# Turning attention queries by 32x32 blocks and on-chip transfers instead of on TensorE (fp32 decoder trunk, one core)

## The chip, the core and the metric

One core of one Trainium2 chip. The metric is the device time of one execution in microseconds; the time before is the median of three runs. Engines are named as the profile names them: PE (TensorE), DVE (VectorE), ACT (ScalarE), POOL (GpSimd) and SP (SyncE, which here only issues transfers).

## The reference, cut to what matters

A decoder trunk on 512 tokens of width 1024 in fp32: one Griffin layer (gated linear recurrence and a SwiGLU), then one layer of dilated attention, and a second SwiGLU. The change lies in the attention layer:

```python
k, v = shared_kv(h, kv_norm, w_kv, k_norm, cos, sin)      # 3 groups x 2 key/value heads x 128

q = (rms_norm(h, b_norm) @ w_q).reshape(B, S, N_GROUPS, Q_HEADS, HEAD_DIM)   # 3 groups x 8 heads x 128
q = rms_norm(q, q_norm[:, None, :])         # over each head's 128
q = apply_partial_rope(q, cos, sin)         # the first 32 of the 128
for g, (window, dilation) in enumerate(((128, 1), (512, 4), (2048, 16))):
    o, l = dilated_window_attention(q[:, :, g], k[:, :, g], v[:, :, g], window, dilation)
wts = softmax(stack(lses)); o = sum(wts * outs)
h = h + o.reshape(B, S, 1024) @ w_o
```

A query meets some 128 keys of each of the three groups, and the groups share one softmax.

## The kernel before

Weights are fp32 and are used as two parts, a high one (rounded to the format fp32r) and a low one (the rest), and so are activations: every product is three matmuls, hi x hi, lo x hi and hi x lo (`mm3`, lines 163 to 165). `Stream` brings the weights in pieces of 128x1024. `_load` issues the load on SP's queue into one of two raw buffers `wr` (line 100). `_split` makes the high part `wh` on ACT (line 117). The low part `wl` comes in one of two ways: for plain pieces DVE subtracts (line 124); for pieces of the kind "dma" ACT writes the weights negated and rounded (line 120) and POOL issues a transfer that adds the weights from memory to them (line 121), which leaves the rest. All 28 pieces of the query weights `w_q` are of the kind "dma" (4 of the 24 are loaded a second time). A load waits until the piece two before it has been split.

`project` goes through four pieces per pass and, with each, over four tiles of 128 tokens: 24 matmuls a piece, 96 a pass (lines 1048 to 1050), and each tile ends in one PSUM bank of 128 tokens x 512 (four heads). Twelve pieces give keys and values. Then `project_q(0)` makes the queries of the first key/value head in three passes (g = 0, 1, 2), pieces 136 to 147 of the stream, and `project_q(1)` those of the second in four (its third pass goes over half the tiles at a time).

For a finished tile `collect` multiplies by the norm's gain (DVE, line 982, into a buffer `kn`), squares (ACT, line 984), sums over each head (DVE, line 985) and queues the rotary step. `normed` computes the norm's factors for the pass and scales each tile (DVE, line 1014). `turn` transposes the four 128x128 heads of a tile on PE (line 1127) into one PSUM bank, and ACT copies the bank into `qt` (line 1129) with the tokens regrouped in four phases. `query_part` splits `qt` into `qh` and `ql` (`halve`: ACT line 279, DVE line 280). These steps are not done at once: `at(n, fn)` sets one n steps later, and `tick()` after each tile of a projection (or each second step of attention) carries out what is due. The order of instructions on each engine is that of the program, with `tc.high_priority()` around the splits and the softmax.

`attend` runs 32 units (2 key/value heads x 4 blocks of 128 tokens x 4 phases). A unit is `scores` (9 matmuls into a bank called S or X), `softmax` (DVE 1192 and 1195, ACT 1200, DVE 1201, POOL 1202), then three units later `turned` (PE transposes, line 1214) and `values`. `plan` says how much of the remaining projection and of the output projection stands between the units; `START_Q` steps of `project_q(1)` come before the first. While `filling[0]` is true all scores use the bank S.

The second SwiGLU and the first already turn their rows without PE, in `land`: DVE transposes 32x32 blocks (line 720), and transfers on SP (12) and POOL (4) put the blocks where they belong (line 730).

Of the kernel before, what the change touches and what calls it, by code (L numbers as in the profile page):

```python
# [15 lines left out]
F32 = mybir.dt.float32  # L16
# [4 lines left out]
ALU = mybir.AluOpType  # L21
# [135 lines left out]
def trunk(tc, A, out):  # L157
# [695 lines left out]


N_TMP = 6
N_KN = 4
STATS = 5
N_PR = 4
LAG = 3
START_Q = 10  # L860


def rotary(nc, A, rp, tp):
# [79 lines left out]
def attention(tc, A, ap, ws, env):  # L943
# [12 lines left out]
    def phases(t):  # L956
        return t.rearrange("q (p n i) -> q p n i", n=4, p=4)

    sph = ap.tile([128, T], F32, name="sph", tag="kn", bufs=N_KN)
# [14 lines left out]
    def collect(raw, nh, j, n, st, tab, g_row):  # L974

        if j == 0:
            st["sq"] = ap.tile([128, n * nh], F32, name="sqc", tag=f"sqc{nh}").rearrange("q (t i) -> q t i", i=nh)
            st["kn"] = []
        dst = ap.tile([128, 512], F32, name="kn", tag="kn", bufs=N_KN)
        rows = raw[:, :128 * nh]  # L980
        x = dst.rearrange("q (h d) -> q h d", d=128)[:, :nh]
        V.tensor_tensor(x, rows.rearrange("q (h d) -> q h d", d=128),
                        grow[:, g_row].unsqueeze(1).to_broadcast([128, nh, 128]), ALU.mult)
# [15 lines left out]
    def normed(st, nh, tab, turn, lag, tiles=range(4)):  # L999

        kn = dict(zip(tiles, st["kn"]))
        first, n = tiles[0], len(tiles)

        def factors():
            sq = st["sq"]
            V.scalar_tensor_tensor(sq, sq, 1.0 / 128.0,
                                   epsv[:, tab + first:tab + first + n].unsqueeze(2).to_broadcast([128, n, nh]),
                                   ALU.mult, ALU.add)
            st["r"] = rsqrt(sq.rearrange("q t i -> q (t i)"), ap, f"qr{nh}")

        def scale(t):
            j = nh * (t - first)
            x = kn[t].rearrange("q (h d) -> q h d", d=128)[:, :nh]
            V.tensor_tensor(x, x, st["r"][:, j:j + nh].unsqueeze(2).to_broadcast([128, nh, 128]), ALU.mult)
# [46 lines left out]
    v2h, v2l = (ap.tile([128, 2, 512], F32R, name=n, tag=n, bufs=1) for n in ("ph", "pl"))  # L1061
    xph, xpl = [], []
    for k in range(KB):
        tags = (("qt", 12), ("qt", 12)) if k < 6 else (("qh", 3), ("ql", 3))
        for lst, src, (tag, bufs), eng in ((xph, xh, tags[0], S.copy), (xpl, xl, tags[1], G.tensor_copy)):
            lst.append(ap.tile([128, T], F32R, name="xp", tag=tag, bufs=bufs))
            eng(phases(lst[k]), by_phase(src[k].bitcast(F32)))
    at(STATS, stats)
    ws.asp = 2
    for g in range(3):  # L1070
# [45 lines left out]
    def project_q(kv):  # L1116

        early, late, every = range(2), range(2, 4), range(4)
        passes = [(0, every), (1, every), (2, early), (2, late)] if kv else [(g, every) for g in range(3)]
        for j, (g, tiles) in enumerate(passes):  # L1120
            def done_q(t, ps, g=g, st={}, tiles=tiles, j=j):
                collect(ps, 4, t - tiles[0], len(tiles), st, t, 3 + g)
                if t == tiles[-1]:
                    def turn(j, rows):
                        pt = bank("X" if kv and g else "PT")
                        for i in range(4):
                            PE.transpose(pt[:, 128 * i:128 * i + 128], rows[:, 128 * i:128 * i + 128], ident)  # L1127
                        q = ap.tile([128, 4, 4, 32], F32, name="qt", bufs=12)
                        S.copy(q, pt.rearrange("q (h p i) -> q p h i", h=4, p=4))
# [19 lines left out]
    def query_part(kv, n, g):  # L1149
# [5 lines left out]
        halve(qt.pop((n, kv, g)).rearrange("q p h i -> q (p h i)"), qh, ql)  # L1155
        qs_[kv, n, g] = qh, ql

    def query_parts(kv, n):
# [134 lines left out]
    for k, u in enumerate(attend()):  # L1293
        for i, (fill, steps, u0, u1) in enumerate(plan):
# [90 lines left out]
```

## Time and profile before

| | |
|---|---|
| Runs | 1169.56, 1167.65, 1168.88 us; median 1168.88 |
| Profiled execution | 1166.22 us, span 1164.4 us, mean granted clock of PE 0.999 |
| PE, PE weight load | 1151.9 us (99%), 952.2 us (82%) |
| DVE, ACT, POOL | 851.5 us (73%), 623.8 us (54%), 186.3 us (16%) |
| First load of query weights, first scaling of queries | 538.4 us, 587.5 us |
| Query transposes on PE, line 1127 | 96, 14.4 us busy |

Times in the profile run from the start of the span. In a group's row, "x96 | 14.4, 274 | 1.4 <-ACT" reads: 96 instructions, busy 14.4 us in all, 274 ns each, and the engine sat idle 1.4 us ahead of them, mostly until that ACT instruction. A row of waits reads: who waited, for whom, us in all, times, longest. A row of a queue gives min/median/max of an issue in ns and the first and last start in us.

### The profile page before, as it was taken

The numbers are of one execution on the slowest core, as the hardware profiler recorded it, in microseconds if no ns is written. First come the engines' busy times: TensorE is split into PE (matmuls) and PEld (weight loads), VectorE is DVE, ScalarE is ACT, GpSimd is POOL, SyncE is SP. The second block draws the span as 40 slices with busy tenths as digits, with TensorE's granted clock in tenths as the row PEclk, the third lists the DMA queues.
The fourth block names the chain that finished last, engine by engine and source line by source line (L and its number), as shares of the span: only waits on it lengthen the run. The fifth ranks groups of instructions, "written<-read, shape, count | busy, mean of one in ns | idle before, by whom it ended". The sixth has DMA issues, their size and how long they took to land.

```text
span 1164.4 us, 15128 instructions
## 1 busy us (share of the span) xinstructions
PE 1151.9 (99%) x5403; PEld 952.2 (82%) x5403; DVE 851.5 (73%) x1525; ACT 623.8 (54%) x901; POOL 186.3 (16%) x221
## 2 busy tenths in 40 slices
PE   9999999999999999999999999999999999999998
PEld 6788888888888888888888888798888888888887
DVE  7988688968777676887565667765988777676864
ACT  6797455543435353565555667665555435353532
POOL 4210010201011000020411334341002011011000
PEclk9999999999999999999999999999999999999999
DMA  7643366966665723433978657534668665757323
GB/s 244 149 114 110 105 225 159 242 193 160 183 164 174 188 73 82 129 107 89 222 182 178 142 113 179 127 73 108 219 160 233 186 165 177 182 162 191 81 71 128
DMA packets 92234, 179.61 MB, mean 154 GB/s; under 512 B 8704, under 2 KB 27008, under 8 KB 92160
## 3 DMA queue, kind: packets, MB, share of 16 engines
q1 hardware_dynamic: 72720, 130.80, 34.6%
q0 software_dynamic: 18864, 47.19, 22.9%
q8 instruction: 43, 0.70, 0.2%
q10 hardware_dynamic: 576, 0.66, 0.2%
q14 instruction: 31, 0.25, 0.1%
HBM read 164.99 MB, written 2.10 MB: 143 GB/s over the span
## 4 chain that ended last, share of the span: by engine, by line
PE 92%; DVE 3%; ACT 2%; issue 1%; DMA 1%; POOL 0%; ACTq 0%; DVEq 0%; SPq 0%
PE ps L165 25%; PE ps L164 25%; PE ps L163 25%; PE ps L1048 5%; PE ps L1049 5%; PE ps L1050 5%; PE ps L1127 1%; PE ps L1214 1%; DVE xc L451 1%; DMA h<-in_x 0%; ACT pr L1200 0%; PE ps L296 0%; DVE ql L280 0%; ACT wh L117 0%; DMA wr<-in_w_in 0%
## 5 line engine op out<-in xcount | busy, mean ns | idle before, releaser
L117 ACT CAST wh<-wr 128x1024 fp32r<-128x1024 f32 (+2 forms) x136 | 131.2, 969 | 136.3 <-PE ps L164 83.1
L164 PE MATMUL ps<-wl,xh 128*128 128x512 f32 x320 | 124.7, 390 | 0.0
L165 PE MATMUL ps<-wh,xl 128*128 128x512 f32 x320 | 124.7, 390 | 0.0
L163 PE MATMUL ps<-wh,xh 128*128 128x512 f32 x320 | 124.7, 390 | 0.0
L165 PE MATMUL ps<-gh,wl 128*128 128x512 f32 x288 | 114.6, 398 | 0.3
L163 PE MATMUL ps<-gh,wh 128*128 128x512 f32 x288 | 113.8, 395 | 0.0
L164 PE MATMUL ps<-gl,wh 128*128 128x512 f32 x288 | 113.7, 395 | 0.0
L124 DVE TENSOR_TENSOR wl<-wr,wh 128x1024 fp32r<-128x1024 f32 (+2 forms) x93 | 100.0, 1083 | 17.4 <-ACT wh L117 17.0
L649 POOL DMA_DIRECT2D S<-in_f_in x40 | 48.2, 1237 | 370.8 <-DMA S<-in_f_in 187.2
L163 PE MATMUL ps<-xh,wh 128*128 128x512 f32 x256 | 101.1, 396 | 0.7 <-ACT xh L274 0.7
L663 ACT CAST wh<-S 128x1024 fp32r<-128x1024 f32 x60 | 63.0, 1050 | 70.4 <-PE ps L165 28.0
L164 PE MATMUL ps<-xl,wh 128*128 128x512 f32 x256 | 100.2, 391 | 0.1
L165 PE MATMUL ps<-xh,wl 128*128 128x512 f32 x256 | 100.0, 391 | 0.0
L664 DVE TENSOR_TENSOR wl<-S,wh 128x1024 fp32r<-128x1024 f32 x60 | 73.2, 1222 | 31.5 <-ACT wh L663 31.5
L163 PE MATMUL ps<-wh,T 128*128 128x512 f32 x240 | 93.6, 390 | 0.0
L165 PE MATMUL ps<-wh,T 128*128 128x512 f32 x240 | 93.6, 390 | 0.0
L164 PE MATMUL ps<-wl,T 128*128 128x512 f32 x240 | 93.5, 390 | 0.0
L1048 PE MATMUL ps<-wh,xh 128*128 128x512 f32 x224 | 91.6, 409 | 0.0
L1050 PE MATMUL ps<-wh,xl 128*128 128x512 f32 x224 | 87.8, 392 | 0.0
L1049 PE MATMUL ps<-wl,xh 128*128 128x512 f32 x224 | 87.4, 390 | 0.0
L781 DVE TENSOR_TENSOR h<-h,ps 128x512 f32<-128x512 f32 x64 | 43.3, 685 | 54.9 <-PE ps L165 54.9
L163 PEld LDWEIGHTS ps<-wh,xh 128*128 128x128 f32 x320 | 60.1, 188 | 12.6
(284 smaller groups left out, 2669.7 us busy)
## 6 DMA issues: line engine op xcount, KB each, us to landing
S<-in_f_in SPq DMA_DIRECT2D x40, 512.0 KB, 6.4
S<-in_f_in POOLq DMA_DIRECT2D x40, 512.0 KB, 8.9
wr<-in_f_out SPq DMA_DIRECT2D x36, 512.0 KB, 5.2
wr<-in_w_q SPq DMA_DIRECT2D x28, 512.0 KB, 6.9
wl<-in_w_q POOLq DMA_DIRECT2D x28, 512.0 KB, 7.6
GA<-in_f_in SPq DMA_DIRECT2D x20, 512.0 KB, 4.9
GB<-in_f_in SPq DMA_DIRECT2D x20, 512.0 KB, 6.9
UB<-in_f_in SPq DMA_DIRECT2D x20, 512.0 KB, 4.9
```

What stands on the lines that cost most here:

```text
L117: nc.scalar.copy(hi[:, c], r[:, c])
L124: a = eng.tensor_tensor(lo[:, c], r[:, c], hi[:, c].bitcast(F32), ALU.subtract)
L163: PE.matmul(ps, wh, xh, start=first, stop=False, skip_group_check=on)
L164: PE.matmul(ps, wh, xl, start=False, stop=False, skip_group_check=on)
L165: PE.matmul(ps, wl, xh, start=False, stop=last, skip_group_check=on)
L649: nc.gpsimd.dma_start(c, p.part(1, q, n == "S1", i), accum_op=ALU.add)
L663: S.copy(hi, r)
L664: V.tensor_tensor(lo, r, hi.bitcast(F32), ALU.subtract)
L781: V.tensor_tensor(by_time(x), by_time(x), in_turn(ps), ALU.subtract)
L1048: PE.matmul(ps[t], xh[k][:, r], wh[:, c], start=k == 0, stop=False)
L1049: PE.matmul(ps[t], xh[k][:, r], wl[:, c], start=False, stop=False)
L1050: PE.matmul(ps[t], xl[k][:, r], wh[:, c], start=False, stop=k == 7)
```

## The change

Four things change together.

1. *Turning.* For queries, `collect` writes its tile with the four heads' 32-wide blocks side by side (block b, head h, 32). `scale_heads` scales on ACT, one instruction for each head (4 per tile, 96 in all). `turn_blocks` transposes the 32x32 blocks of a tile on DVE in place (24). When the second tile of a pair is done, `turn` issues 16 transfers from SBUF to SBUF for the pair: each takes 32 partitions x 2 tiles x 128 values (32 KB), 12 on SP's queue and 4 on POOL's. Twelve pairs make 144 and 48. The 96 PE transposes, the 24 ACT copies out of PSUM and the 24 DVE scalings are gone. `query_part(0, 0, g)` is set eight steps behind the transfers.
2. *Buffers.* `kn` and `qt` hold pairs: `kn` has two buffers of two tiles (before, four of one), `qt` six of two (before, twelve of one).
3. *Low parts.* Of the first twelve pieces of `w_q` every second one gets its low part by DVE's subtraction: six ACT passes and six accumulating POOL transfers go, six DVE subtractions come.
4. *Order.* `START_Q` is 13, not 10; the third pass of `project_q(0)` is normalised in halves; `filling[0]` ends with the first entry of `plan`, so that scores alternate between S and X from there on.

```diff
-    p_q = add_pieces([A["w_q"][i] for i in (*range(24), *range(20, 24))], "dma")
+    p_q = add_pieces([A["w_q"][i] for i in range(12)], "dma", 2)
+    add_pieces([A["w_q"][i] for i in (*range(12, 24), *range(20, 24))], "dma")
...
-N_KN = 4
+N_KN = 2
...
-START_Q = 10
+START_Q = 13
...
-        dst = ap.tile([128, 512], F32, name="kn", tag="kn", bufs=N_KN)
+        if j % 2 == 0:
+            st["pairs"].append(ap.tile([128, 2, 512], F32, name="kn", tag="kn", bufs=N_KN))
+        dst = st["pairs"][-1][:, j % 2]
...
+            x = dst.rearrange("q (b h d) -> q b h d", b=4, h=nh)
+            V.tensor_tensor(x, rows.rearrange("q (h b d) -> q b h d", b=4, h=nh),
+                            g.rearrange("q (b d) -> q b d", b=4).unsqueeze(2).to_broadcast([128, 4, nh, 32]), ALU.mult)
...
+        def scale_heads(t):
+            x = kn[t].rearrange("q (b h d) -> q h b d", b=4, h=nh)
+            for i in range(nh):
+                j = nh * (t - first) + i
+                S.activation(x[:, i], x[:, i], AF.Copy, scale=st["r"][:, j:j + 1])
+
+        def turn_blocks(t):
+            blocks = kn[t].rearrange("q (k i) -> q k i", i=32)
+            V.transpose(blocks, blocks)
+            if t % 2:
+                turn(t - 1, st["pairs"][(t - first) // 2])
...
-            at(2 + j, lambda t=t: scale(t))
-            at(lag + j, lambda t=t: turn(t, kn[t]))
+            if lag:
+                at(2 + j, lambda t=t: scale(t))
+                at(lag + j, lambda t=t: turn(t, kn[t]))
+            else:
+                at(2 + j, lambda t=t: scale_heads(t))
+                at(3 + j, lambda t=t: turn_blocks(t))
...
+                if not kv and g == 2:
+                    tiles = (early, late)[t // 2]
...
-                    def turn(j, rows):
-                        pt = bank("X" if kv and g else "PT")
-                        for i in range(4):
-                            PE.transpose(pt[:, 128 * i:128 * i + 128], rows[:, 128 * i:128 * i + 128], ident)
-                        q = ap.tile([128, 4, 4, 32], F32, name="qt", bufs=12)
-                        S.copy(q, pt.rearrange("q (h p i) -> q p h i", h=4, p=4))
-                        qt[j, kv, g] = q
-                        if not kv and not j:
-                            query_part(0, 0, g)
-
-                    normed(st, 4, 0, turn, {3: 7}.get(j, 8), tiles)
+                    def turn(n, rows):
+                        q = ap.tile([128, 2, 4, 128], F32, name="qt", tag="qt", bufs=6)
+                        src = rows.rearrange("q n (b x) -> q n b x", b=4)
+                        for p in range(4):
+                            for b in range(4):
+                                (G if p == 3 else nc.sync).dma_start(q[32 * b:32 * b + 32, :, p],
+                                                                     src[32 * p:32 * p + 32, :, b])
+                        for i in range(2):
+                            qt[n + i, kv, g] = q[:, i]
+                        if not kv and not n:
+                            at(8, lambda: query_part(0, 0, g))
+
+                    normed(st, 4, 0, turn, None, tiles)
...
+                if i == 0 and given[i] == steps:
+                    filling[0] = False
                 if i == 1 and given[i] == steps:
                     move()
-                if i == 2 and given[i] == steps:
-                    filling[0] = False
```

What stands where on the engines that wait or are waited for: SP's queue where the first two query groups are turned (`wr146` is the load of piece 146), before:

```order
L100 DMA wr144_5063<-in_w_q 128x1024
L100 DMA wr145_5108<-in_w_q 128x1024
L100 DMA wr146_5191<-in_w_q 128x1024
L100 DMA wr147_5230<-in_w_q 128x1024
L100 DMA wr148_5279<-in_w_q 128x1024
L100 DMA wr149_5324<-in_w_q 128x1024
L100 DMA wr150_5407<-in_w_q 128x1024
L100 DMA wr151_5446<-in_w_q 128x1024
```

and in the changed program:

```order
L100 DMA wr145_5111<-in_w_q 128x1024
L1163 DMA qt_4995<-kn_4891 32x2x128 x12
L1163 DMA qt_5042<-kn_4922 32x2x128 x12
L100 DMA wr146_5192<-in_w_q 128x1024
L100 DMA wr147_5262<-in_w_q 128x1024
L100 DMA wr148_5311<-in_w_q 128x1024
L100 DMA wr149_5346<-in_w_q 128x1024
L100 DMA wr150_5448<-in_w_q 128x1024
L1163 DMA qt_5229<-kn_5125 32x2x128 x12
L1163 DMA qt_5276<-kn_5156 32x2x128 x12
L100 DMA wr151_5528<-in_w_q 128x1024
```

Two blocks of 24 transfers now stand in the row of loads, the first ahead of `wr146`, the second ahead of `wr151`.

PE at the beginning of attention, where the names `kh` and `kl` (4011 to 4013 for the three groups) mark the scores of a unit (9 rows each) and lines 1048 to 1050 (1075 to 1077 in the changed program) the projection. Before, projection follows on the first unit's last scores:

```order
L163 MATMUL ps<-kh_4012,qh 128x64
L164 MATMUL ps<-kl_4018,qh 128x64
L165 MATMUL ps<-kh_4012,ql 128x64
L163 MATMUL ps<-kh_4013,qh 128x64
L164 MATMUL ps<-kl_4019,qh 128x64
L165 MATMUL ps<-kh_4013,ql 128x64
L1048 MATMUL ps<-wh_5409,xh 128x512
L1049 MATMUL ps<-wl_5410,xh 128x512
L1050 MATMUL ps<-wh_5409,xl 128x512
```

In the changed program the first unit's last scores are followed by those of the second and the third:

```order
L163 MATMUL ps<-kh_4013,qh 128x64
L164 MATMUL ps<-kl_4019,qh 128x64
L165 MATMUL ps<-kh_4013,ql 128x64
L163 MATMUL ps<-kh_4011,qh 128x128
L164 MATMUL ps<-kl_4017,qh 128x128
L165 MATMUL ps<-kh_4011,ql 128x128
L163 MATMUL ps<-kh_4012,qh 128x64
L164 MATMUL ps<-kl_4018,qh 128x64
L165 MATMUL ps<-kh_4012,ql 128x64
L163 MATMUL ps<-kh_4013,qh 128x64
L164 MATMUL ps<-kl_4019,qh 128x64
L165 MATMUL ps<-kh_4013,ql 128x64
```

The projection between the first units has moved ahead of them, and three units follow on one another in the bank S.

DVE where a group of queries ends: in the changed program the turning of the pairs `kn_4891` and `kn_4922` stands here ahead of the gain multiplication of the next group, into a pair that takes the buffer of `kn_4891` (`wl144` is the low part of piece 144, by subtraction):

```order
L1035 STREAM_TRANSPOSE kn_4891<-kn_4891 128x512 x2
L1035 STREAM_TRANSPOSE kn_4922<-kn_4922 128x512
L124 TENSOR_TENSOR wl144_5080<-wr144_5077,wh144_5079 128x1024
L1035 STREAM_TRANSPOSE kn_4922<-kn_4922 128x512
L992 TENSOR_TENSOR kn_5125<-ps_4964,grow_1855 128x512
L281 TENSOR_TENSOR ql_5102<-qt_4995,qh_5101 128x512
```

The multiplication in the fifth row is new behind the transfers out of `kn_4891`.

More of the change, by code (lines that the diff above doesn't have):

```diff
@@ L957, in phases @@
         return t.rearrange("q (p n i) -> q p n i", n=4, p=4)
-    sph = ap.tile([128, T], F32, name="sph", tag="kn", bufs=N_KN)
+    sph = ap.tile([128, 2 * T], F32, name="sph", tag="kn", bufs=N_KN)[:, :T]
     G.tensor_copy(phases(sph), by_phase(ssum))
@@ L976, in collect @@
         if j == 0:
-            st["sq"] = ap.tile([128, n * nh], F32, name="sqc", tag=f"sqc{nh}").rearrange("q (t i) -> q t i", i=nh)
-            st["kn"] = []
-        dst = ap.tile([128, 512], F32, name="kn", tag="kn", bufs=N_KN)
-        rows = raw[:, :128 * nh]
-        x = dst.rearrange("q (h d) -> q h d", d=128)[:, :nh]
-        V.tensor_tensor(x, rows.rearrange("q (h d) -> q h d", d=128),
-                        grow[:, g_row].unsqueeze(1).to_broadcast([128, nh, 128]), ALU.mult)
+            st["sq"] = ap.tile([128, 16], F32, name="sqc", tag=f"sqc{nh}")[:, :n * nh].rearrange(
+                "q (t i) -> q t i", i=nh)
+            st["kn"], st["pairs"] = [], []
+        if j % 2 == 0:
+            st["pairs"].append(ap.tile([128, 2, 512], F32, name="kn", tag="kn", bufs=N_KN))
+        dst = st["pairs"][-1][:, j % 2]
+        rows = raw[:, :128 * nh]
+        g = grow[:, g_row]
+        if nh == 2:
+            x = dst.rearrange("q (h d) -> q h d", d=128)[:, :nh]
+            V.tensor_tensor(x, rows.rearrange("q (h d) -> q h d", d=128),
+                            g.unsqueeze(1).to_broadcast([128, nh, 128]), ALU.mult)
+        else:
+            x = dst.rearrange("q (b h d) -> q b h d", b=4, h=nh)
+            V.tensor_tensor(x, rows.rearrange("q (h b d) -> q b h d", b=4, h=nh),
+                            g.rearrange("q (b d) -> q b d", b=4).unsqueeze(2).to_broadcast([128, 4, nh, 32]), ALU.mult)
+            x = x[:, 0]
         S.activation(rows, rows, AF.Square)
@@ L1063, in attention @@
     for k in range(KB):
[L1064 to L1067, printed above, removed]
+        if k < 6:
+            pair = ap.tile([128, 2, T], F32R, name="xp", tag="qt", bufs=6)
+            homes = [pair[:, i] for i in range(2)]
+        else:
+            homes = [ap.tile([128, T], F32R, name="xp", tag=tag, bufs=3) for tag in ("qh", "ql")]
+        for lst, src, home, eng in ((xph, xh, homes[0], S.copy), (xpl, xl, homes[1], G.tensor_copy)):
+            lst.append(home)
+            eng(phases(home), by_phase(src[k].bitcast(F32)))
     at(STATS, stats)
@@ L1120, in project_q, with done_q @@
         for j, (g, tiles) in enumerate(passes):
[L1121 removed]
+            def done_q(t, ps, g=g, sts=({}, {}), tiles=tiles):
+                if not kv and g == 2:
+                    tiles = (early, late)[t // 2]
+                st = sts[tiles == late]
                 collect(ps, 4, t - tiles[0], len(tiles), st, t, 3 + g)
                 if t == tiles[-1]:
[L1124 to L1134 removed]
+                    def turn(n, rows):
[10 more added lines that the diff above has]
+                    normed(st, 4, 0, turn, None, tiles)
             yield from project(p_q + 12 * kv + 4 * j, xh, xl, done_q, tiles)
@@ L1154, in query_part @@
         qh, ql = [ap.tile([128, 512], F32R, name=x, tag=x, bufs=tags[2]) for x in tags[:2]]
-        halve(qt.pop((n, kv, g)).rearrange("q p h i -> q (p h i)"), qh, ql)
+        halve(qt.pop((n, kv, g)).rearrange("q p x -> q (p x)"), qh, ql)
         qs_[kv, n, g] = qh, ql
```

1 line of the change is left out of this document (added).

## The prediction

> **What bounds the kernel now.** I read the page's head and its chain first (which engine ends last), then PE's waits, then the windows of the stretch in which the queries are made, then the rows of the queues that the change touches.
>
> ```profile
> span 1164.4 us, 15128 instructions
> PE 1151.9 (99%) x5403; PEld 952.2 (82%) x5403; DVE 851.5 (73%) x1525; ACT 623.8 (54%) x901; POOL 186.3 (16%) x221
> ...
> PE 92%; DVE 3%; ACT 2%; issue 1%; DMA 1%; POOL 0%; ACTq 0%; DVEq 0%; SPq 0%
> ```
>
> PE is busy 99% of the span and carries 92% of the chain: an instruction taken from PE shortens the time by its own length, unless PE then waits. The windows (PE, PEld, DVE, ACT, POOL busy, clock, DMA share, GB/s) show where there is room for new waits:
>
> ```profile
> 580.00:600.00 20.00, 20.00 (x97) 16.59 (x96) 10.20 (x32) 10.77 (x15) 2.58 (x3) 1.00 0.86 198
> 660.00:680.00 20.00, 19.44 (x124) 16.96 (x123) 10.36 (x37) 11.58 (x24) 7.62 (x6) 1.00 0.63 128
> 700.00:720.00 20.00, 18.22 (x120) 15.95 (x119) 12.67 (x37) 14.45 (x25) 8.20 (x6) 1.00 0.74 165
> 720.00:740.00 20.00, 19.04 (x128) 16.82 (x126) 15.08 (x48) 17.25 (x33) 8.27 (x7) 1.00 0.71 159
> ```
>
> At 580 to 600 (projection of the first queries alone) PE never stops and DVE and ACT are half free; from 660 on attention is woven in, POOL works, and PE idles a little. The second row of this fence shows PE's waits on what the change replaces:
>
> ```profile
> PE ps L1127 <- ACT qt L1129: 1.3, 2, 1.0
> ...
> PE ps L163 <- ACT qt L1129: 1.2, 1, 1.2
> ```
>
> **Removed from PE.** 96 transposes and those waits. Their own row gives 14.4 us; what they cost in the pipe I take from the collecting pass, which is periodic, and from the matmuls inside it.
>
> ```profile
> L1127 PE MATMUL ps<-ident,kn 128*128 128x128 f32 x96 | 14.4, 274 | 1.4 <-ACT qt L1129 1.3
> ...
> 601.13 0.69 DVE L982 TENSOR_TENSOR kn<-ps,grow 128x512 f32<-128x512 f32 x1 [7.64 <-PE ps L1050]
> 624.78 0.69 DVE L982 TENSOR_TENSOR kn<-ps,grow 128x512 f32<-128x512 f32 x1 [7.64 <-PE ps L1050]
> ...
> 605.23 0.39 PE L1049 MATMUL ps<-wl,xh 128*128 128x512 f32 x1
> 614.30 0.40 PE L1050 MATMUL ps<-wh,xl 128*128 128x512 f32 x1
> ```
>
> One pass (96 matmuls and 16 transposes) lasts 624.78 - 601.13 = 23.65 us. The last two rows are the first and the last of 41 back-to-back matmuls: 9.07 / 40 = 0.227 us each, so 96 take 21.77 and 16 transposes 1.88. Six passes' worth: **-11.3 us** (14.4 is the other end). The waits: 1.3 + 1.2 = **-2.5**. Together -13.8. A piece of weights (24 matmuls) is then 5.44 us of PE.
>
> **Moved on ACT, DVE, POOL.**
>
> ```profile
> L120 ACT ACTIVATE wl<-wr 128x1024 fp32r<-128x1024 f32 x26 | 27.6, 1060 | 16.7 <-PE ps L1049 16.6
> ...
> L1014 DVE TENSOR_TENSOR kn<-kn,qr4y 128x512 f32<-128x512 f32 x24 | 15.7, 706 | 0.2
> ...
> L1129 ACT COPY qt<-ps 128x512 f32<-128x512 f32 x24 | 13.7, 581 | 15.4 <-PE ps L1127 15.2
> ...
> L279 ACT CAST kh<-ps 128x128 fp32r<-128x128 f32 x24 | 6.3, 265 | 8.5 <-DVE kl L280 4.9 <-PE ps L1102 3.6
> ...
> L720 DVE STREAM_TRANSPOSE wt<-e 128x512 f32<-128x512 f32 x40 | 25.9, 687 | 0.0
> ...
> L124 DVE TENSOR_TENSOR wl<-wr,wh 128x1024 fp32r<-128x1024 f32 x71 | 85.9, 1220 | 13.8 <-ACT wh L117 13.6
> ```
>
> ACT loses 24 copies (13.9) and 6 low-part passes (6.4) and gains 96 scalings of 128x128, at the nearest row's 0.265: +25.4, net +5.1 us over some 190. DVE loses 24 scalings (16.9) and gains 24 transposes (16.5) and 6 subtractions (7.3), net +6.9. POOL loses 6 accumulating transfers and gains 48 small ones. I cost all three at nothing while projection runs alone, since DVE and ACT are half idle there; at 720 to 740 ACT has 2.75 of 20 us left, and if that cover fails the 16 scalings per pass show: that is in the last term below. The two buffers of paired rows mean that DVE's gain multiplication of the next group waits until the last pair has landed; queued behind it are the low parts of piece 146 on, which PE reaches at 581.3 + 6 x 5.44 = 614, and PE has other banks until then.
>
> **Added to SP: the term that decides.** Twelve pairs, each 12 transfers on SP and 4 on POOL, go into the queue that also carries the weight loads, in order.
>
> ```profile
> L730 SPq DMA_DIRECT2D gl<-wt x96: 591/599/927, 227.3 to 1087.7; - x96
> ...
> L730 POOL DMA_DIRECT2D gl<-wt x32: 549/572/608, 227.9 to 1082.7; - x32
> DMA to landing us min/median/max: 2.0/2.2/3.8
> ```
> ```profile
> 227.30 8.11 SPq L730 DMA_DIRECT2D gl<-wt  x12
> 235.45 0.59 SPq L93 DMA_DIRECT2D wr<-in_f_out  x1
> ```
> ```profile
> L647 SPq DMA_DIRECT2D S<-in_f_in x40: 367/462/3014, 157.7 to 1047.6; - x40
> ```
> ```profile
> L93 SPq DMA_DIRECT2D wr<-in_f_out x36: 367/469/2145, 158.8 to 1121.5; - x36
> ```
>
> The nearest transfers in kind (L730, on chip, four 512-byte runs on each of 32 partitions) take 0.60 each, 0.64 with the gap. The new ones have two runs on each of 32. The row nearest in that is L647, two runs per partition, median 0.46. Bounds of c, one issue with its gap: 0.37 (its minimum) to 0.64. I take c = 0.50, L647's median and L730's gap of 0.04, because runs per partition are what the two rows differ in beside the place.
>
> When do they start? ACT's row below marks the start of piece 140 (581.3), which ends the first query group; DVE has the factors at 587.5:
>
> ```profile
> 581.33 1.06 ACT L120 ACTIVATE wl<-wr 128x1024 fp32r<-128x1024 f32 x1 [0.23 <-PE ps L1049]
> ...
> 587.51 2.50 DVE L1014 TENSOR_TENSOR kn<-kn,qr4y 128x512 f32<-128x512 f32 x4
> ```
>
> Two tiles scaled on ACT (8 x 0.265), the second one's DVE transpose (0.69) and 0.8 of gaps put the first transfer at 591.1. A group's 24 transfers take 24c, and the loads of pieces 146 and 147 stand behind them (146 is one of the six whose low part DVE now subtracts, with no transfer; it is there in time). Then each load waits for the split of the load two before it: 146, 148, 150, then the second group's 24 transfers, then 151. With L from issue to landing of a load, A the same for an accumulating low part, and 8.3 for splits and issues between them (two on ACT, 2.1, three times; the POOL issue, 0.9; gaps, 1.1), piece 151 is ready at 591.1 + 48c + 3L + A + 8.3. PE wants it at 581.3 + 11 x 5.44 = 641.2.
>
> ```profile
> wr<-in_w_q SPq DMA_DIRECT2D x28, 512.0 KB, 6.9
> wl<-in_w_q POOLq DMA_DIRECT2D x28, 512.0 KB, 7.6
> ...
> wr<-in_w_kv SPq DMA_DIRECT2D x12, 512.0 KB, 3.5
> ```
> ```profile
> L121 POOL DMA_DIRECT2D wl<-in_w_q x28: 860/874/1382, 548.7 to 722.5; - x28
> ...
> DMA to landing us min/median/max: 5.8/7.4/9.8
> ```
>
> L lies between 3.5 (loads alone) and 6.9 (with accumulates beside them); behind a pause of the loads it is between, 5.2. A: between its minimum 5.8 and its median 7.4, 6.6. So 591.1 + 24 + 15.6 + 6.6 + 8.3 = 645.6 less 641.2: near **+4.4** of stalls up to there (none at c = 0.37 with L = 4, 17.0 at c = 0.64 with the medians).
>
> **Scores in one bank.** Attention begins three steps later, with the turned queries eight steps behind their transfers. By the order, the first three units' scores come late and back to back in one PSUM bank (before, projection lay between). PE waits twice until DVE has read the bank:
>
> ```profile
> 707.50 0.42 DVE pr L1192
> 707.97 0.48 DVE pr L1195
> ```
>
> 0.9 each, **+1.8** (0 if the rest hides it). **Later blocks** stand between loads whose pieces last longer, since attention lies between them; with ACT's lost cover I take **+1.5**, half of 0 to 3.
>
> **Sum.** -13.8 + 4.4 + 1.8 + 1.5 = -6.1. The profiled execution is 1166.2 (span 1164.4), so 1160.1; it lies 2.7 below the median 1168.9, to which I compare: **about 1163**. 0.2% (2.3 us) is what a measurement of this kernel can tell.
>
> The Trainium skill, "VectorE: DVE Perf Modes", section "Rules for kernel authors", speaks against the change: a 128x128 transpose belongs on TensorE if PSUM may take the result, since VectorE turns only 32x32 blocks. The price of the detour is here the transfers; the rival of a full SP queue below is that rule's outcome.
>
> **Rivals.**
> 1. *All hidden.* c near 0.37 and L near 4: piece 151 is ready at 591.1 + 17.8 + 12 + 6.6 + 8.3 = 635.8, before PE wants it. -13.8 with 0 to 1.8 for the scores: some 1156. For it: L647's minimum, and loads that land in 3.5 when alone. Against: that row's median, 0.46.
> 2. *Cancelled.* c = 0.55 with L = 6.2: 651.0, a stall of 9.8; with 1.8 and 1.5 the sum is -0.7: 1168.
> 3. *The SP queue becomes the bound (slower).* The transfers cost what L730 costs (0.64), since both are on chip, and loads land in 6.2: 591.1 + 30.7 + 18.6 + 7.0 + 8.3 = 655.7, a stall of 14.5; later blocks 3, scores 1.8: +5.5, 1174. It decides from a stall of about 10.5 at piece 151 on. For it: L730's minimum and median are alike, so its price does not look like a queue's. Against: the load right behind L730's twelve took as long, 0.59, where its like (L93) takes 0.47 in the median, so part of the price is the queue's.
>
> A stall in one piece of over 3.4 us would by the Trainium skill ("TensorE: Matmul & The Clock Gate", Part 1) halve PE's clock for about as long. No window above has such a gap (clock 1.00 with 1.78 us idle in 20). In rival 3 two such stalls would, as an estimate from that page, add some 3 us.
>
> That the change does not do what it says is not open: the 96 transposes are gone from PE's order.
>
> **Chances.** Likeliest (1159 to 1166.5): 0.35. All hidden (below 1159): 0.24. Cancelled (within 0.2%): 0.18. SP's queue (above 1171.2): 0.23. Faster 0.35 + 0.24 = 0.59. The range leaves out a tenth at each end: 1154.5 (everything hidden and the transposes nearer 14.4) to 1174. The likeliest one's own range is 1159 to 1166.5.
>
> **What would show it.** PE's row of transposes on the identity for queries gone, and a pass of 21.8 us where projection runs alone; SP's row of the new transfers at 0.46 (0.33 for rival 1, 0.60 for rival 3); PE waiting on the low parts of pieces 147 to 151 for 3 to 6 us in all; waits of scores on DVE of about 1.8; PE's clock still 1.00. The prediction is wrong if the new transfers cost 0.6 and PE does not wait (the loads have more slack than I give them), or if PE waits for the turned queries or for ACT at 700 to 760.

## The result: 3.1% slower

The changed kernel takes 1204.2 us in the median (1202.4 to 1205.5) beside 1168.3 for the kernel before: ratio 1.0307, 95% interval 1.0288 to 1.0327. Forecast was 1163, with 1174 as the upper end. In the experiments below, one execution each of e5 and e8 took 4070 and 3468 us, and their medians leave it out. The page of the profiled execution (span, busy times, PE's granted clock in 40 slices, the chain):

```profile
span 1200.5 us, 15374 instructions
...
PE 1161.7 (97%) x5307; PEld 955.9 (80%) x5307; DVE 859.5 (72%) x1540; ACT 631.6 (53%) x967; POOL 208.3 (17%) x263
...
PEclk9999999999999999999998799799999999999999
...
PE 79%; issue 5%; DVE 4%; SPq 4%; DMA 4%; ACT 2%; POOL 1%; ACTq 0%; DVEq 0%; POOLq 0%
```

The span grew by 36.1 us, and two rows split it. PE's idle time (span less busy) went from 12.5 to 38.8: +26.3. PE's busy time went up by 9.8 although 96 transposes, 11.3 us by the prediction's price, are gone: the remaining matmuls took 21.1 us longer. 26.3 + 21.1 - 11.3 = 36.1. The clock row shows why matmuls took longer. Before, it was 9 in every slice:

```profile
PEclk9999999999999999999999999999999999999999
```

The mean granted clock agrees: 0.982 beside 0.999, and 0.017 of 1200.5 us is 20 us. The same in windows (PE, PEld, DVE, ACT, POOL busy, clock, DMA share, GB/s), first two of before, then the changed kernel's:

```profile
620.00:640.00 20.00, 20.00 (x93) 16.56 (x92) 11.80 (x37) 10.06 (x14) 2.58 (x3) 1.00 0.80 179
640.00:660.00 20.00, 20.00 (x115) 17.24 (x114) 11.48 (x45) 14.15 (x25) 5.55 (x6) 1.00 0.60 138
```

```profile
600.00:620.00 20.00, 17.91 (x78) 14.21 (x77) 11.00 (x35) 7.16 (x12) 1.47 (x2) 1.00 0.55 135
620.00:640.00 20.00, 15.30 (x56) 11.81 (x56) 6.56 (x14) 11.32 (x23) 7.17 (x11) 0.83 0.83 182
640.00:660.00 20.00, 15.00 (x62) 12.00 (x62) 10.35 (x38) 11.68 (x24) 5.94 (x9) 0.90 0.69 181
660.00:680.00 20.00, 15.90 (x57) 13.23 (x57) 9.72 (x36) 7.72 (x14) 3.88 (x5) 0.68 0.65 159
680.00:700.00 20.00, 20.00 (x123) 17.54 (x123) 11.70 (x46) 14.27 (x36) 12.12 (x15) 1.00 0.49 104
...
760.00:780.00 20.00, 16.27 (x90) 14.57 (x90) 10.54 (x34) 10.65 (x21) 5.15 (x6) 0.70 0.49 114
```

Where PE had never stopped before (580 to 660) it now idles up to a quarter of the time, and four of the windows shown run at 0.68 to 0.90 of the clock. Where it loses, counted by the start of a piece's first matmul on PE (a pass of queries is four pieces):

| start of piece | 140 | 144 | 148 | 151 | 152 | 156 | 159 | 160 | 163 |
|---|---|---|---|---|---|---|---|---|---|
| before, us | 581.4 | 605.0 | 628.7 | 647.9 | 655.5 | 692.8 | 713.1 | 717.3 | 737.7 |
| after, us | 582.0 | 603.8 | 634.9 | 652.1 | 674.1 | 711.7 | 730.9 | 744.0 | 773.1 |

One pass after the first goes as predicted (21.8 us). Then come three losses: by piece 148, at the first scores (151 to 152), and from 159 on, where the second head's last queries are made. What PE waited for in the changed kernel (us in all, times, longest):

```profile
PE ps L1076 <- DMA wl<-in_w_q: 10.6, 3, 5.0
PE ps L163 <- ACT qh L280: 7.8, 4, 3.3
PE ps L163 <- DVE mn L1231: 6.0, 3, 2.8
PE ps L1075 <- DVE sqc L996: 2.7, 3, 1.5
```

Low parts that come late, queries that come late, and a DVE that comes late. Behind all three stand the new transfers, as e1 will show (rows of their line: issue min/median/max, who waited for them, time to land):

```profile
L1163 SPq DMA_DIRECT2D qt<-kn x144: 585/595/1810, 592.7 to 796.9; - x144
L1163 POOL DMA_DIRECT2D qt<-kn x48: 542/559/619, 593.2 to 791.8; - x48
...
  DVE kn L992: 41.3, 7
  ACT qh L280: 21.5, 4
...
DMA to landing us min/median/max: 1.8/3.3/8.9
```

An issue costs 0.595, as much as L730's with twice the runs. SP's queue by time shows the two blocks in the row of loads:

```profile
592.66 17.70 SPq L1163 DMA_DIRECT2D qt<-kn  x24
610.41 12.86 SPq L100 DMA_DIRECT2D wr<-in_w_q  x5
624.40 19.28 SPq L1163 DMA_DIRECT2D qt<-kn  x24
643.79 8.76 SPq L100 DMA_DIRECT2D wr<-in_w_q  x4
```

24 issues last 17.7 and 19.3 us, 0.74 and 0.80 each: beyond the issue's median price, some single issues take longer (up to 1.81 in the row) and SP waits within a block.

### The profile page after: what moved, and what is told of

Its sections match the earlier page's. It is cut to its first block, busy times and chain, and to the rows that moved or that the text cites. A ratio compares the mean times of both kernels' runs of the same rounds, so it can differ in the third digit from the quotient of the medians.

```text
span 1200.5 us, 15374 instructions
## 1 busy us (share of the span) xinstructions
PE 1161.7 (97%) x5307; PEld 955.9 (80%) x5307; DVE 859.5 (72%) x1540; ACT 631.6 (53%) x967; POOL 208.3 (17%) x263
## 4 chain that ended last, share of the span: by engine, by line
PE 79%; issue 5%; DVE 4%; SPq 4%; DMA 4%; ACT 2%; POOL 1%; ACTq 0%; DVEq 0%; POOLq 0%
PE ps L165 23%; PE ps L164 22%; PE ps L163 22%; SPq L1163 4%; PE ps L1075 3%; PE ps L1076 3%; PE ps L1077 3%; DMA qt<-kn 2%; DVE xc L452 1%; DMA wl<-in_w_q 1%; ACT kn L1031 1%; DMA wl<-in_w_in 1%; PE ps L1250 1%; ACT wh L117 0%; DVE xp L442 0%
## 5 line engine op out<-in xcount | busy, mean ns | idle before, releaser
L164 PE MATMUL ps<-wl,xh 128*128 128x512 f32 x320 | 124.6, 389 | 0.0
L165 PE MATMUL ps<-wh,xl 128*128 128x512 f32 x320 | 124.5, 389 | 0.0
L124 DVE TENSOR_TENSOR wl<-wr,wh 128x1024 fp32r<-128x1024 f32 (+2 forms) x99 | 107.3, 1092 | 23.1 <-ACT wh L117 22.9
L1076 PE MATMUL ps<-wl,xh 128*128 128x512 f32 x224 | 91.9, 410 | 10.6 <-DMA wl<-in_w_q 10.6
L664 ACT CAST wh<-S 128x1024 fp32r<-128x1024 f32 x60 | 63.0, 1050 | 70.3 <-PE ps L165 27.9
L1077 PE MATMUL ps<-wh,xl 128*128 128x512 f32 x224 | 91.3, 407 | 0.0
```

The costliest lines, as they stand in the source:

```text
L124: a = eng.tensor_tensor(lo[:, c], r[:, c], hi[:, c].bitcast(F32), ALU.subtract)
L164: PE.matmul(ps, wh, xl, start=False, stop=False, skip_group_check=on)
L165: PE.matmul(ps, wl, xh, start=False, stop=last, skip_group_check=on)
L664: S.copy(hi, r)
L1076: PE.matmul(ps[t], xh[k][:, r], wl[:, c], start=False, stop=False)
L1077: PE.matmul(ps[t], xl[k][:, r], wh[:, c], start=False, stop=k == 7)
```

## The experiments

Three theories. *SP order*: loads stand behind the transfers, so low parts come late. *Buffers*: DVE waits 41 us for a pair's buffer until its transfers have landed, and everything behind it on DVE is late. *Landing*: the transfers share the DMA engines with loads and accumulating low parts of 512 KB and end late, whoever waits. The rival to all three: ACT's scaling or the new order cost it. Each ratio below is to the kernel before, run beside the experiment (medians 1166.3 to 1167.1).

**e1, one transfer per pair.**

```diff
-                        for p in range(4):
-                            for b in range(4):
-                                (G if p == 3 else nc.sync).dma_start(...)
+                        nc.sync.dma_start(q.rearrange("q n p x -> q n (p x)"), rows)
```

> The changed kernel with one transfer per pair of tiles (128 partitions, 256 KB, SP) in place of the sixteen; the blocks are then not moved across partitions, so the queries are left in the wrong order. All else stays: scaling on ACT, transposes on DVE, half of the low parts, the order. If the sixteen issues are the cause (in whatever queue or wait), about 1155 to 1159, below the kernel before, as the sum without the SP term gives. If ACT's scaling, DVE's transposes or the new order are the cause, over 1185.

1168.2, ratio 1.0009 (0.9998 to 1.0021). So the sixteen transfers in place of one are the whole loss of 3%, but the expected gain is missing too. Its page, its waits of PE and the row of its transfers on SP:

```profile
span 1166.2 us, 15052 instructions
...
PE 1147.3 (98%) x5307; PEld 946.2 (81%) x5307; DVE 859.2 (74%) x1540; ACT 631.6 (54%) x967; POOL 180.5 (15%) x215
```
```profile
PE ps L163 <- ACT qh L280: 3.5, 3, 1.8
PE ps L163 <- ACT ph L280: 2.5, 2, 2.3
PE ps L1076 <- DMA wl<-in_w_q: 2.2, 1, 2.2
```
```profile
L1160 SPq DMA_DIRECT2D qt<-kn x12: 465/471/550, 592.2 to 756.2; - x12
```

Up to piece 159 it is 11 us ahead of the kernel before (702.1 beside 713.1); at 163 it is 1.7 behind (739.4). In between PE waits for ACT, twice by some 2 us. An issue costs 0.471 here: this transfer too stays on chip, but goes over all 128 partitions and moves nothing from one partition to another.

**e2, loads on ACT's queue.**

```diff
-                itertools.zip_longest(..., fillvalue=self.nc.sync)]
+                itertools.zip_longest(..., fillvalue=self.nc.scalar if i in self.other else self.nc.sync)]
...
+        ws.other = range(p_q + 8, p_o + 8)
```

> The changed kernel with the loads of pieces 144 on (query and output weights) issued by ACT's queue, so that no load stands behind a transfer on SP. Theory SP order (late loads make PE wait for low parts, and its clock falls with the waits): most of the 36 us comes back, 1168 to 1180, and PE no longer waits on DMA wl. Theory buffers (DVE waits 41 us for a pair's buffer until its transfers have landed, and the next queries come late): the transfers keep their 18 to 19 us per group, so 1195 or more.

1210.6, ratio 1.0370 (1.0349 to 1.0391): no gain at all. The wait on low parts is nearly gone (0.7 us), and others took its place (lines are one or two further down here):

```profile
PE ps L164 <- ACT qh L282: 21.1, 4, 8.5
PE ps L1077 <- DVE sqc L998: 10.6, 5, 5.2
...
PE ps L1078 <- DMA wl<-in_w_q: 0.7, 1, 0.7
```

So the theory of SP's order, which was the prediction's, is not the cause alone. The run is not a clean test of it: 28 loads of 0.33 us now stand in ACT's own row, ahead of splits that PE waits for.

**e3, half of the transfers on POOL.**

```diff
-                                (G if p == 3 else nc.sync).dma_start(...)
+                                (G if p >= 2 else nc.sync).dma_start(...)
```

> The changed kernel with 8 of a pair's 16 transfers on POOL's queue instead of 4. SP then needs 16 x 0.75 = 12 us for a group instead of 18 to 19, POOL 16 x 0.57 = 9. Both theories, SP order and buffers, expect about half of the 36 us back: 1182 to 1192; if transfers on POOL hold back the accumulating low parts and the scaling of the softmax, 1200 or more.

1202.7, ratio 1.0301 (1.0281 to 1.0321), within the interval of the changed kernel. Neither theory's number came, but the third outcome did (1200 or more), with twice the transfers on POOL; whether POOL's other work is what they held back, the run does not show. DVE still waits 29.8 us for transfers, ACT 20.8, and PE's wait for queries grew from 7.8 to 20.0.

**e4, the rest of the change alone** (the kernel before, with these lines):

```diff
-    p_q = add_pieces([A["w_q"][i] for i in (*range(24), *range(20, 24))], "dma")
+    p_q = add_pieces([A["w_q"][i] for i in range(12)], "dma", 2)
+    add_pieces([A["w_q"][i] for i in (*range(12, 24), *range(20, 24))], "dma")
...
-START_Q = 10
+START_Q = 13
...
+                if i == 0 and given[i] == steps:
+                    filling[0] = False
...
-                if i == 2 and given[i] == steps:
-                    filling[0] = False
```

> The kernel before with the rest of the change alone: half of the low parts of the first twelve pieces by DVE, START_Q 13, scores in two banks from the first entry of the plan on. Turning on PE, scaling on DVE as before. If the turning is the cause of the loss, within 4 us of the kernel before, 1164 to 1172; if the order or the low parts are, over 1175.

1168.3, ratio 1.0009 (0.9999 to 1.0018): these parts of the change neither help nor harm. (The third pass normalised in halves is not among them; e1 has it.)

**e5 and e12, the rows freed early.**

```diff
...
-                                                                     src[32 * p:32 * p + 32, :, b])
+                                    src[32 * p:32 * p + 32, :, b] if b == 0 and p in (0, 3) else
+                                    grow[32 * p:32 * p + 32, 0:2])
```

> The changed kernel with all 192 transfers, but 14 of a pair's 16 read a constant instead of the turned rows (so the queries are wrong), and the pair's buffer is free for the next group once two transfers have landed. SP's queue, the landing times and ACT's wait for the landed queries stay. Theory buffers (DVE's 41 us of waiting for a pair's buffer is what delays the rest): DVE's wait for transfers falls below 15 us and most of the 36 us comes back, 1175 to 1185. Theory landing (the queries and loads come late because issues and landings are slow, whoever waits): 1195 or more.

> The run in which 14 of a pair's 16 transfers read a constant, once more for its profile. Theory buffers: DVE's wait for transfers is below 15 us (41 in the changed kernel), and PE reaches piece 148 near 628 instead of 635; ACT's wait for the landed queries (21 us) is still there.

e5: 1187.8, ratio 1.0185 (1.0169 to 1.0201); e12, a single run of 1190.2, gives the profile. DVE's wait is gone and ACT's is halved:

```profile
  ACT qh L280: 11.2, 3
  DVE kn L992: 2.8, 1
```

14 to 16 of the 36 us come back. Piece 148 starts at 631.6, not at 628. One reservation: since most transfers no longer depend on the rows, 11 of them were issued at 542 and one load slipped between two blocks, so the run also eases SP's order a little. PE's wait on low parts stays (11.3 us beside 10.6).

**e6, no accumulating transfers for query weights** (both `add_pieces` of `w_q` without "dma").

> The changed kernel with the low parts of all query weights by DVE's subtraction, so no accumulating transfer (22 of 512 KB before) shares the DMA engines with the new transfers. Theory landing: the transfers land in 2 to 2.5 us in the median instead of 3.3, PE's wait on DMA wl is gone, ACT's and DVE's waits for transfers fall by a third or more: 1180 to 1190. If the number of issues alone sets the time: 1198 to 1206. If DVE, with 27 us more work, becomes late: above 1206.

1192.9, ratio 1.0226 (1.0210 to 1.0242). The transfers land in 1.9 us:

```profile
  DVE kn L992: 19.3, 5
  ACT qh L280: 18.8, 5
...
DMA to landing us min/median/max: 1.7/1.9/4.3
```

11 us come back; DVE waits half as long. The accumulating transfers are a cause. Through landing alone this is not shown: the run also takes PE's 10.6 us of waits on low parts away and 18.8 us off ACT's busy time (631.6 to 612.8).

**e7, one transfer per pair and the scaling on DVE** (`scale_heads` as one multiplication per tile with the factors broadcast).

> The run with one transfer per pair, with the scaling moved back from ACT (96 instructions) to DVE (24). That run gained 11 us up to piece 159 and lost them between 700 and 740, where ACT was waited for. If ACT's added work is what took the gain: PE waits less on ACT there, 1156 to 1161. If it is something else (DVE, the second late half group, the clock after a wait): 1165 to 1171.

1163.8, ratio 0.9973 (0.9961 to 0.9985): 4.4 less than e1, the first run below the kernel before, between the two expectations. ACT's added work is part of the missing gain. Part of the rest is in the clock: the executions with a mean granted clock of 0.999 took 1160.3 to 1162.8, those with 0.992 to 0.997 took 1163.5 to 1166.1. The one wait on a low part in the profiled execution, and the windows from there:

```profile
PE ps L1076 <- DMA wl<-in_w_q: 2.1, 1, 2.1
```
```profile
697.00:700.00 3.00, 0.88 (x4) 0.41 (x3) 3.00 (x8) 2.00 (x3) 2.23 (x2) 1.00 0.99 229
700.00:704.00 4.00, 4.00 (x19) 3.56 (x18) 4.00 (x9) 1.41 (x3) 0.41 (x1) 0.57 1.04 303
704.00:708.00 4.00, 4.00 (x30) 3.68 (x30) 1.16 (x6) 2.73 (x5) 2.72 (x2) 1.00 0.97 315
```

After 2.1 us of waiting PE does 19 matmuls in 4 us, then 30.

**e8, three passes early** (the kernel before; passes named in `BLOCKED` go by 32x32 blocks, four tiles in one set of 16 transfers of 64 KB).

```diff
+BLOCKED = ((0, 0), (0, 1), (1, 0))
...
+                        if blocked:
+                            q = qt_all[:, 4 * g:4 * g + 4].rearrange("q n (p x) -> q n p x", p=4)
+                            for p in range(4):
+                                for b in range(4):
+                                    (G if p == 3 else nc.sync).dma_start(q[32 * b:32 * b + 32, :, p],
+                                                                         src[32 * p:32 * p + 32, :, b])
```

> The kernel before with three of the seven query passes turned by DVE and transfers (both first passes of the first key/value head and the first of the second, whose queries are needed 20 us or more later), four tiles in one set of 16 transfers (64 KB each) instead of two sets per four tiles; the other passes stay on PE; half of the low parts of the first twelve pieces by DVE. 48 transposes less on PE are worth 5.6 us. If what costs is the number of issues ahead of loads and the shortness of time until the queries are needed, 1161 to 1165. If any block of transfers in the row of loads costs PE more than 2 us, 1168 to 1175.

1180.6, ratio 1.0114 (1.0098 to 1.0131), above both outcomes. Here the second head's first pass lands in slots that the first head still uses, so part of the attention is computed with the wrong queries; e9 leaves that pass out.

**e9, two passes early** (`BLOCKED = ((0, 0), (0, 1))`, slots apart, scaling on DVE).

> The kernel before with only two of the seven query passes turned by DVE and transfers, those whose queries wait longest (the first and second of the first key/value head), a whole pass of four tiles in one set of 16 transfers of 64 KB, scaling left on DVE, and half of the low parts of the first twelve pieces by DVE; all other passes on PE. 32 transposes less are worth 3.8 us. If a set of 12 issues on SP (7.7 us) between loads hides and the queries are not waited for: 1162 to 1165. If the pass after it waits for the buffer of the rows, and PE with it: 1168 to 1174.

1177.2, ratio 1.0096 (1.0081 to 1.0111). With two sets of 12 issues on SP the kernel is 10.6 us slower than before: the second outcome, and more than it named. DVE waits once for each set:

```profile
DVE kn L987 <- DMA qt<-kn: 15.9, 1, 15.9
DVE kn L991 <- DMA qt<-kn: 11.4, 1, 11.4
```

**e10, half as many issues, same bytes.**

```diff
-                        for p in range(4):
+                        for p in (0, 2):
...
+                                (G if p and b > 1 else nc.sync).dma_start(
+                                    q[32 * b:32 * b + 32, :, p:p + 2],
+                                    src[32 * p:32 * p + 32, :, min(b, 2):min(b, 2) + 2])
```

> The changed kernel with 8 transfers per pair instead of 16, each of two neighbouring blocks (64 KB; one of the two ends in a wrong place, so the queries are wrong). Bytes as before, half the issues. If the number of issues sets the loss, about half of it comes back beyond what one transfer per pair showed (1168 at 12 issues, 1204 at 192): near 1186. If the bytes or the time to land set it: 1198 or more.

1179.7, ratio 1.0113 (1.0092 to 1.0135):

```profile
L1163 SPq DMA_DIRECT2D qt<-kn x72: 585/596/1932, 591.8 to 768.7; - x72
...
  DVE kn L992: 4.6, 1
...
DMA to landing us min/median/max: 2.0/4.1/6.2
```

Twice the bytes per transfer, the same price of an issue. 12 issues 1168, 96 issues 1180, 192 issues 1204: the number counts, and the second half costs twice the first. The transfers land later than in the changed kernel (4.1 us in the median beside 3.3), and still DVE's wait for them falls from 41.3 us to 4.6. That points to the length of a block of issues, and not to the landing of one transfer, as what holds DVE.

**e11, e5 and e6 together.**

> The changed kernel with both removals at once: 14 of a pair's 16 transfers read a constant (the queries are wrong), so the rows' buffer is free early, and the low parts of all query weights come from DVE without accumulating transfers. Alone they gave back 15 and 11 us. If they act in different places (DVE's wait, landing of the loads and low parts): 1176 to 1181. If both only shorten the same chain (transfers that end late): 1184 to 1190.

1173.0, ratio 1.0059 (1.0042 to 1.0076): 31 us back, more than 15 + 11 and below both outcomes. A reading that would fit is that the two causes feed each other: a transfer that lands late holds DVE, which makes the next rows, the next low parts and the next transfers late. No run shows that chain by itself.

**e13, e11 with the scaling on DVE.**

> The run with the rows freed early and no accumulating transfers (1173; the queries are wrong, 14 of 16 transfers read a constant), with the scaling on DVE as well. All 192 issues remain. If ACT's scaling is the rest that stood above the kernel before (it was worth 4.4 us where one transfer per pair was left): 1166 to 1170, so three causes make up the 36 us. If the issues on SP themselves cost the rest: 1171 to 1175.

1174.8, ratio 1.0080 (1.0065 to 1.0095): no gain, the second outcome.

**e15, the changed kernel with the scaling on DVE.**

> The changed kernel with the scaling on DVE, 24 instructions, instead of 96 on ACT; nothing else. If ACT's time counts here as in the runs with one transfer per pair: 1199 to 1201. If the transfers set the time and hide it: 1202 to 1206.

1201.1, at the border of the two outcomes; ratio 1.0302 (1.0286 to 1.0318), within the interval of the changed kernel. ACT's scaling cost something only in the run with one transfer per pair. What keeps e11 and e13 above the kernel before may then be the 144 issues ahead of the loads (ACT waits 15.1 us for weight loads in e11, 20.7 in e13); that was not isolated.

**e14, e9 with the low parts of the first 16 query pieces by DVE** (no accumulating transfer near the two sets).

> The run with two early passes turned by DVE and transfers, with the low parts of the first 16 pieces of query weights by DVE, so that no accumulating transfer stands before or beside the two sets of transfers. There they landed up to 8 us after their issue and DVE waited 16 and 11 us for the rows' buffer. If the landing behind 512 KB transfers is the cause: DVE waits below 8 us each, PE does not wait on DMA wl, 1162 to 1167. If one buffer of rows for a whole pass is too few in any case: 1170 or more.

1171.3, ratio 1.0043 (1.0030 to 1.0055). Up to piece 148 everything works: 624.6 beside 628.7 before, the worth of 32 transposes. Then one wait of DVE for the second set (8.6 us) reaches PE, the second outcome. Here the row of PE:

```profile
PE ps L1074 <- DVE sqc L995: 5.4, 1, 5.4
```

**e16, a single early pass** (`BLOCKED = ((0, 0),)`, the first ten query pieces by DVE).

> The kernel before with a single query pass (the first) turned by DVE and one set of 16 transfers of 64 KB, and the low parts of the first ten pieces of query weights by DVE, so that no accumulating transfer runs beside it. 16 transposes less on PE are worth 1.9 us: 1164 to 1166 if the set hides, 1168 or more if DVE's wait for the rows' buffer reaches PE even here.

1175.8, ratio 1.0081 (1.0067 to 1.0095). Even with one set of 12 issues on SP the kernel is 9.5 us slower than before. PE waits twice, for the low parts of pieces 146 and 147, the first that take the long way (ACT, POOL, landing):

```profile
PE ps L1075 <- DMA wl<-in_w_q: 6.8, 2, 3.9
```

ACT makes 146's negated weights 4.1 us late, waiting for a transfer; those of 147 then wait 8.6 us for PE, which still uses their buffer. The order of the program also moved some of piece 146 ahead of the last tiles of 144 and 145, so it was wanted early. e14, in which both pieces take the short way, has no such wait; a set in SP's row seems to cost where low parts have the long way behind it, though in e16 the changed order has a part in it that was not separated.

**e17, e14 with the sets dealt to three queues.**

> The run with two early passes and no accumulating transfers near them (1171; PE lost 5.4 us once, while DVE waited 8.6 us for the second set), with a set's 16 transfers dealt to SP, POOL and ACT (6, 5, 5) instead of 12 and 4. A set is then issued in 4 us instead of 8. If the length of the set is what PE waited for: the wait falls to 2 us or less and the time to 1163 to 1167. If it is the late start of the set (DVE's low parts wait for loads): 1169 to 1172.

1171.2, ratio 1.0035 (1.0022 to 1.0048): two waits of 2.4 us in place of one of 5.4, and no gain: the length of the set on SP is not what is left. No version with transfers of the right blocks beat the kernel before.

## Why the prediction was wrong, step by step

1. *PE's gain* held: one pass took 21.8 us (582.0 to 603.8), and e14 had 4.1 us by piece 148 where 3.8 was the price of two passes.
2. *The issue, c = 0.50*, is the term mis-sized first. The row chosen as nearest by runs (L647) was the wrong one; L730's price, 0.60, is that of every transfer here that takes 32 partitions to 32 others: 0.595 with 64 runs, 0.596 with 64 longer ones (e10), 0.599 with 128. To be on chip is not enough: e1's transfer over 128 partitions took 0.471, close to L647's 0.46. With waits inside the block it was 0.74 to 0.80 per issue, 17.7 us for the first 24 where the sum had 12.
3. *Piece 151.* The sum said 4.4 us late. Piece 151 started at 652.1 beside the 641.2 that the sum took as due, 10.9 late, then PE waited 5.0 more for its low part: 15.9 in all, beside 14.5 in the third rival. Most of the 10.9 was lost before piece 148, where the sum had no stall: DVE held PE for some 2 us, and the low part of piece 147, which the sum did not follow, came 4.1 late. The mechanism up to here is in the main the predicted one; e2 shows that taking it away does not free the time while the others are there.
4. *What lies behind piece 151 is the step that failed.* Without any stall the sum's own 13.8 would have made the profiled execution 1152.4; it took 1202.4. Of these 50 us some 16 lie before the low part of piece 151, and some 34 behind it, where the sum had 3.3 (1.8 for the scores, 1.5 for *later blocks*). The later blocks were priced as late loads and ACT's lost cover. What the sum left out is "The two buffers ... PE has other banks until then", costed at nothing. DVE's row:

```profile
L992 DVE TENSOR_TENSOR kn<-ps,grow 128x512 f32<-128x512 f32 x24 | 16.1, 687 | 45.3 <-DMA qt<-kn 41.3 <-PE ps L1077 2.6 <-PE ps L1076 1.4
```

Every gain multiplication is the first of a chain on DVE (rotary, sums, factors, transposes, the next transfers, low parts, the scores' maxima), so what waits there makes the next block late as well. e5 and e12 bring some 15 us back by freeing the rows early, e10 24.5 by halving the issues. How the rest of the 34 us divides among landing, the issues themselves and the clock is not separated.

5. *Landing* of the transfers: the prediction showed L730's 2.2 and gave it no term. It was 3.3 in the median and 8.9 at worst with the accumulating transfers beside them, 1.9 and 4.3 without (e6, which brought 11 us back, not by landing alone). ACT, which splits the landed queries, waits 21.5 us, with the next pieces' splits and the exponentials behind it.
6. *ACT's scaling* was priced by a cast out of PSUM, 0.265; it took 0.389, 30.0 us rather than 25.4:

```profile
L1031 ACT ACTIVATE kn<-kn,qr4y 128x128 f32<-128x128 f32 x96 | 30.0, 389 | 9.1 <-DVE qr4y L271 9.1
```

Taking it off ACT helped in one case, with one transfer per pair (e1 to e7, 4.4 us).

7. *The clock.* The prediction let it drop only after a gap of 3.4 us, in one rival, for 3 us in all, and expected it to stay at 1.00. It cost 21.1 us. PE's rows around the first long wait (start, length; the starts are 0.43 apart, then 0.23):

```profile
627.27 0.80 PE L1076 MATMUL ps<-wl,xh 128*128 128x512 f32 x1 [4.10 <-DMA wl<-in_w_q]
...
630.85 0.63 PE L1075 MATMUL ps<-wh,xh 128*128 128x512 f32 x1
631.27 0.63 PE L1076 MATMUL ps<-wl,xh 128*128 128x512 f32 x1
...
632.33 0.40 PE L1076 MATMUL ps<-wl,xh 128*128 128x512 f32 x1
632.57 0.40 PE L1077 MATMUL ps<-wh,xl 128*128 128x512 f32 x1
```

A wait of 4.1 us is followed by 4.8 at about half speed (0.43 instead of 0.23 for each matmul, 2.3 us lost): it costs 6.4 us, not 4.1.

The third rival had the right sign, and its price of 0.64 (issue and gap) was the right one; up to piece 151 its stall was right within 1.4 us, in part by luck, since most of that time was lost earlier and at other waits. It gave 1174 because behind that piece it added 4.8 us where some 34 came: DVE and ACT, too, wait in order for the transfers (41.3 and 21.5 us), and waits of PE are charged again by the clock. The prediction's own signs of being wrong came in part: PE waited for the turned queries (7.8 us, the longest of 3.3 at 764). The Trainium skill ("VectorE: DVE Perf Modes", "Rules for kernel authors") leaves a 128x128 transpose to TensorE, and this case agrees: 16 transposes cost 1.9 us of PE, the cheapest detour found (e17) 0.35% of the kernel.

## What to carry to other kernels

Price a new transfer by the row that moves data between partitions in the same way, not by its runs, and count issues, not bytes. For each buffer that now stays held until a transfer lands, follow the engine that waits for it in order, and all that stands behind; a wait that looks harmless on an idle engine is not when that engine also makes the next transfer's data. Where PE is busy all the time, a wait of 2 us can cost it about 4 (2.1 and 1.7 in e7), though it does not always (e1).

## What the runs showed of the hardware

- PE's clock can fall after shorter waits than expected: 0.57 in the 4 us behind a wait of 2.1 us (e7). It does not always: in e1 a wait of 2.15 us left it at 1.00 in the next 5 us. The waits of 1.2 us and less in the kernel before, from 580 us on, left it at 1.00, as did one of 1.5 in the changed kernel (window 600 to 620). The Trainium skill ("TensorE: Matmul & The Clock Gate", Part 1) names an idle window of about 3.4 us; in e7 a shorter wait was enough.
- On SP the price of an on-chip transfer from 32 partitions to 32 others did not depend on its size: 0.595 for 32 KB, 0.596 for 64 KB in 64 runs, 0.599 for 64 KB in 128 runs. One of 256 KB over all 128 partitions took 0.471 (e1), a load of 512 KB 0.33.
- The transfers of 32 KB landed in 3.3 us in the median (8.9 at worst) with accumulating transfers of 512 KB beside them, in 1.9 (4.3) without them (e6).
